# Norms of the heads' outputs: repeated over the channels by products, or as rows that a DMA repeats

## The chip, the cores and the metric

The kernel runs on one core of a Trainium2 chip. The metric is device time in microseconds of one execution. The engines that matter are TensorE (PE, with its weight loads as PEld), VectorE (DVE), ScalarE (ACT), GpSimd (POOL) and SyncE (SP), which here does nothing but issue DMAs, in the order of its queue.

## The reference, cut to what matters

A block with two layers over 768 tokens: 512 latent ones and 256 of a context, 1024 channels wide. Each layer projects a normed input into four groups of four heads each (windowed attention with a sink, "swa"; retention, "ret"; RWKV-7, "rwkv"; latent attention, "mla"), joins their outputs, projects them with `w_out`, and runs an MLP. The outputs of the retention and RWKV heads go through a norm over the 64 channels of each head, and this is what the change touches:

```python
def head_norm(o, gain, eps):
    mu = jnp.mean(o, axis=-1, keepdims=True)
    var = jnp.mean(jnp.square(o - mu), axis=-1, keepdims=True)
    y = (o - mu) * lax.rsqrt(var + eps)
    return y.reshape(o.shape[:-2] + (-1,)) * gain.astype(jnp.float32)
...
    def finish(o, gate):                                    # retention
        y = head_norm(o.transpose(0, 2, 1, 3), gn_g, RET_EPS)
        return (y * jax.nn.silu(gate.astype(jnp.float32))).astype(gate.dtype)
```

The kernel has the mean taken out of the weights beforehand, so only the factor rsqrt(mean of squares + eps), one number for each head and token, is left to be made and multiplied in.

## The kernel before

**Stages.** For each layer `l` the class Block runs `mixers` (projections and the RWKV recurrence), `attention` (L653), `out` (the product with `w_out`) and `mlp`. Data lies with channels on the partitions (two heads of 64 channels to a tile of 128 partitions) and tokens along the row. Layer 0 works on six tiles of 128 tokens, layer 1 on the four latent ones.

**What sets the order.** The program is recorded in the order in which it is written, and a scheduler then orders each engine's instructions, with the written order as priority. `merge` (L112) interleaves generators: it always advances the one whose yielded costs are the smallest share of the total that was given for it. In `attention` three streams run so: `mla` (total 58000), `swa` (54000), and `rest` (44000; all three times 0.84 in layer 1). `rest` is a chain: `finish` of RWKV (two pairs of heads, p = 0, 1), `ret` (two pairs, hp = 0, 1), and `w_out(l, 0)`, which loads the first half of the columns of `w_out` in eight pieces of 256 KB into the two buffers called wraw and splits each into a high and a low part, `wo` (an ACT cast at L209 and a subtraction by DVE or POOL at L212). `out` does the same for the second half. The yields of `rest` sum to 44200 in layer 0.

**PSUM.** In this stage there are two single banks (`pr`) and three pairs of banks (`ptok`); `done` gives one back. Three token tiles of the product with `w_out` are under way at a time, one in each pair.

**The norm.** `head_rstd` (L242) takes the squares `sq` of a pair of heads (`fsq` in `finish`, `rsq` in `ret`). `head_sums` sums them over each head by products with a 128x2 selector, scales on DVE (L237) and raises to the power -0.5 on POOL (L239): `hr`, tokens on the partitions, 2n columns for n token tiles. Then `on_channels` (L249) brings each column to 64 partitions by a product: a column of `hr`, broadcast to 64, as the stationary operand, and the identity as the moving one. That is 2n products into a pair of banks, for two `finish` and two `ret` pairs in each layer, 80 products in all (12 to each of four calls in layer 0, 8 to each in layer 1). DVE reads the result from PSUM right behind: at L1775 in `finish` and at L1032 in `ret`.

**Names.** `hrr` is a tile for transposed norms, `rstd` a DRAM row that `normalise` (L1438) already uses in the `mixers` stage: transpose, copy, DMA to DRAM, and DMAs that read each row back to 64 partitions. `prob` and `pt` are the probabilities of both attentions and their transposes, `y` the inputs of `w_out`. "D" is a pool of 17 tiles of 128x2x768, "B" one of 16 of 128x1024. `gate`, `gain` and `x` are rows that `out` needs behind its product. PE records each fp32 product as two.

## Time and profile before

| | us |
|---|---|
| median of 3 runs | 2207.34 (2202.97 to 2211.09) |
| the profiled execution: its own time | 2198.7 |
| the profiled execution: its span | 2196.9 |
| PE busy | 2057.8 (94%) |
| DVE busy | 1297.1 (59%) |
| ACT busy | 808.9 |
| POOL busy | 634.8 |
| mean granted clock of TensorE | 0.977 of full speed |

All stage times below are taken in the profiled execution, whose own time is 1.8 us over its span and 8.6 us under the median. Its first layer's `attention` streams run from 453 to 634.7 us and its product with `w_out` from there to 704 us; the second layer's run from 1630 to 1781.7 us and to 1824 us.

### The profile page before, as it was taken

Reading aid. Unit: us, or ns where it says so; the run is one execution under the profiler, and the core shown is the slowest. Engines: PE = TensorE matmul, PEld = TensorE weight load, DVE = VectorE, ACT = ScalarE, POOL = GpSimd, SP = SyncE. Lnnn points to the kernel's source line nnn. Section 1 sums busy time; section 2 is a strip of 40 time slices with the busy share of each in tenths; the row PEclk is TensorE's granted clock in tenths of the full one; section 3 lists DMA queues with packets and bytes.
Section 4 is the critical chain, followed back from the end, with each engine's and each line's share of the span. In section 5 each row is a group of like instructions: output and inputs, shape, how many; then the busy total and the mean of one; then the engine's idle time right before and its main releaser. Section 6 shows DMA issues by size and latency. Waiting matters only on the chain. (4 is left out here: it accounts for less than half of the span.)

```text
span 2196.9 us, 36212 instructions
## 1 busy us (share of the span) xinstructions
PE 2057.8 (94%) x14420; PEld 1616.1 (74%) x14420; DVE 1297.1 (59%) x2256; ACT 808.9 (37%) x1504; POOL 634.8 (29%) x679
## 2 busy tenths in 40 slices
PE   7988999988999999999999898999998899999997
PEld 4865766656768888888888677566666677888886
DVE  5478687677755756656555655666566645333334
ACT  3244444354444422222221333444454444322321
POOL 2542333331123311112211354333341123222321
PEclk9999999989899999999999999999998999999999
DMA  7233333522134444444443422111341133322332
GB/s 275 81 119 97 104 112 106 159 81 87 30 109 145 142 136 148 134 139 138 129 128 103 154 80 87 55 51 59 92 136 36 63 121 129 114 88 91 103 113 96
DMA packets 110885, 239.88 MB, mean 109 GB/s; under 512 B 22834, under 2 KB 49276, under 8 KB 110716
## 3 DMA queue, kind: packets, MB, share of 16 engines
q1 hardware_dynamic: 110716, 237.57, 33.5%
q8 instruction: 113, 1.85, 0.3%
q14 instruction: 56, 0.46, 0.1%
HBM read 206.93 MB, written 30.58 MB: 108 GB/s over the span
## 5 line engine op out<-in xcount | busy, mean ns | idle before, releaser
L150 PE MATMUL ps<-y,whi 128*128 128x512 f32 (+1 forms) x1664 | 420.9, 342 | 3.6 <-POOL y L493 2.3
L150 PE MATMUL ps<-whi,f 128*128 128x512 f32 x1280 | 399.5, 390 | 3.3 <-DVE f L1202 3.3
L209 ACT CAST whi<-wraw 128x1024 fp32r<-128x1024 f32 (+1 forms) x176 | 182.5, 1042 | 589.6 <-PE ps L150 364.6
L150 PE MATMUL ps<-hT,whi 128*128 128x512 f32 (+3 forms) x1360 | 381.4, 363 | 2.7 <-POOL hT L493 1.2
L150 PEld LDWEIGHTS ps<-y,whi 128*128 128x128 f32 x1664 | 289.0, 189 | 44.1 <-POOL y L493 4.1
L150 PE MATMUL ps<-y,wlo 128*128 128x512 f32 (+1 forms) x832 | 282.8, 341 | 0.6 <-POOL wlo L212 0.6
L150 PEld LDWEIGHTS ps<-whi,f 128*128 128x128 f32 x1280 | 240.2, 188 | 57.3 <-DVE f L1202 4.1
L150 PEld LDWEIGHTS ps<-hT,whi 128*128 128x128 f32 (+1 forms) x1360 | 234.8, 190 | 64.1 <-issue 24.3
L212 POOL TENSOR_TENSOR wlo<-wraw,whi 128x1024 fp32r<-128x1024 f32 x57 | 142.0, 2491 | 434.6 <-ACT whi L209 344.8
L150 PE MATMUL ps<-wlo,f 128*128 128x512 f32 x640 | 249.3, 390 | 0.0
L212 DVE TENSOR_TENSOR wlo<-wraw,whi 128x1024 fp32r<-128x1024 f32 x117 | 149.9, 1284 | 163.0 <-ACT whi L209 162.9
L150 PE MATMUL ps<-hT,wlo 128*128 128x512 f32 (+1 forms) x648 | 232.6, 359 | 0.0
L426 DVE SCALAR_TENSOR_TENSOR aacc<-aw,sil,aacc 128x768 f32<-128x768 f32 x140 | 159.8, 1188 | 30.1 <-ACT aacc L424 20.5
L150 PEld LDWEIGHTS ps<-y,wlo 128*128 128x128 f32 x832 | 157.3, 189 | 18.8 <-POOL wlo L212 0.8
L1201 POOL TENSOR_TENSOR fr<-fr 128x768 f32<-128x768 f32 (+1 forms) x64 | 91.3, 1427 | 271.3 <-ACT f L1200 263.1
L150 PEld LDWEIGHTS ps<-hT,wlo 128*128 128x128 f32 x648 | 124.8, 193 | 22.0 <-issue 7.2
L150 PEld LDWEIGHTS ps<-wlo,f 128*128 128x128 f32 x640 | 120.2, 188 | 24.4
L1202 DVE TENSOR_TENSOR f<-fr,f 128x768 fp32r<-128x768 f32 (+1 forms) x64 | 63.5, 992 | 121.4 <-POOL fr L1201 121.4
L1228 DVE TENSOR_TENSOR ya<-ya,ps 128x1024 f32<-128x1024 f32 x60 | 73.1, 1218 | 98.6 <-PE ps L150 98.6
L150 PE MATMUL ps<-wo,y 128*128 128x512 f32 x480 | 118.2, 398 | 2.9 <-POOL wo L212 2.7
L150 PEld LDWEIGHTS ps<-wo,y 128*128 128x128 f32 x480 | 87.7, 188 | 25.9 <-POOL wo L212 6.0
L1676 POOL TENSOR_SCALAR T<-rwvt 64x128 f32<-64x128 f32 x96 | 61.6, 643 | 74.1 <-PE ps L150 68.3
(306 smaller groups left out, 3231.2 us busy)
## 6 DMA issues: line engine op xcount, KB each, us to landing
wraw<-in_w_b_dram SPq DMA_DIRECT2D x64, 512.0 KB
wraw<-in_mlp_w_dram SPq DMA_DIRECT2D x64, 512.0 KB
aw<-in_ada_w_dram SPq DMA_DIRECT2D x80, 384.0 KB
wraw<-in_w_in_b_dram SPq DMA_DIRECT2D x46, 512.0 KB
ada<-in_ada_w_dram SPq DMA_DIRECT2D x64, 192.0 KB
adaw<-in_ada_s_dram SPq DMA_DIRECT2D x16, 512.0 KB
wraw<-in_w_out_k_dram SPq DMA_DIRECT2D x32, 256.0 KB
xs<-x SPq DMA_DIRECT2D x16, 512.0 KB
```

The costliest lines, as they stand in the source:

```text
L150: ins = self.nc.tensor.matmul(ps, lhsT, rhs, start=start, stop=stop, **kw).ins
L209: ins = self.nc.scalar.copy(hi, src)
L212: (lo_eng or self.nc.vector).tensor_tensor(lo, src, hi.bitcast(F32), ALU.subtract)
L426: nc.vector.scalar_tensor_tensor(a, w, sil, a, ALU.mult, ALU.add)
L1201: nc.gpsimd.tensor_tensor(fr, fr, fr, ALU.mult)
L1202: nc.vector.tensor_tensor(fl, fr, fh.bitcast(F32), ALU.subtract)
L1228: nc.vector.tensor_tensor(ya[t], ya[t], ps, ALU.add)
L1676: nc.gpsimd.tensor_scalar(T3[r, par, dr], self.vt[r, gc[dr]], 1.0, None, ALU.mult)
```

## The change

`head_rstd` no longer calls `on_channels`. It transposes `hr` by one product into a single bank, copies that to `hrr` on ACT, writes it to a DRAM row, and reads the row back twice, each time repeated over 64 partitions, into the tile that held the squares. The users of the norm become functions `last`, put on a list `ends`, and are emitted later: by `end()` in `finish` behind the squares of the next pair, in `ret` behind the token-major copy of v of the next pair, and for the last pair by `at_end()`, which comes behind `w_out(l, 0)`. The yields change (1500 more in each `head_rstd`, less elsewhere), so `rest` sums to 48200, with its total left at 44000.

```diff
@@ -239,12 +239,23 @@
         nc.gpsimd.tensor_tensor(r, r, self.mhalf[:, 0:1].broadcast_to([128, 2 * nt * nb]), ALU.pow)
         return r
 
-    def head_rstd(self, sq, tiles, mul, add, add_op):
-
-        n = len(tiles)
+    def head_rstd(self, sq, tiles, mul, add, add_op, name):
+
+
+        n, t0 = len(tiles), 128 * tiles[0]
         r = self.head_sums([sq], tiles, mul, add, add_op)
         yield 400.0 * n
-        return self.on_channels(lambda j, t: r[:, n * j + t - tiles[0]:n * j + t - tiles[0] + 1], 2, tiles)
+        pt = self.pr(128)
+        self.tp(pt[0:2 * n], r, self.cc("ident"))
+        rr = self.mp.tile([24, 128], F32, tag="hrr", name="hrr", bufs=1)
+        self.nc.scalar.copy(rr[0:2 * n], pt[0:2 * n])
+        self.done(pt)
+        dd = self.dr.tile([2, 128 * n], F32, name=name)
+        self.nc.sync.dma_start(dd.rearrange("r (t x) -> (r t) x", x=128), rr[0:2 * n])
+        for j in range(2):
+            self.nc.sync.dma_start(sq[64 * j:64 * j + 64, t0:t0 + 128 * n], dd[j].partition_broadcast(64))
+        yield 1500.0
+        return sq[:, 0:T]
 
     def on_channels(self, col, n, tiles):
 
@@ -653,9 +664,19 @@
     def attention(self, l, emit):
         merge((self.rw.tail(), 16.0), (self.mla_prep(l, emit), 14e3), (self.swa_prep(l, emit), 4e3))
         self.rebank(2, (2, 4, 6))
-        rest = chain(self.rw.finish(), self.ret(l, emit), self.w_out(l, 0))
+        self.ends = []
+        rest = chain(self.rw.finish(), self.ret(l, emit), self.w_out(l, 0), self.at_end())
         streams = [(self.mla(l, emit), 58000.0 * (1.0 if emit else 0.84)), (self.swa(l, emit), 54000.0 * (1.0 if emit else 0.84)), (rest, 44000.0 * (1.0 if emit else 0.84))]
         merge(*streams)
+
+    def end(self):
+
+        while self.ends:
+            self.ends.pop(0)()
+
+    def at_end(self):
+        self.end()
+        yield 1
 
     def ypair(self, key):
         self.y[key] = self.D("y", F32R)
@@ -952,6 +973,11 @@
         ch = lambda x: x.rearrange("p (c i) -> p c i", i=128)
         rep = lambda x: x.unsqueeze(1).broadcast_to([128, nch, 128])
         cjx = lambda x: x.rearrange("p (c j x) -> p c j x", j=2, x=64)
+
+        def last(hp, o, rs):
+            nc.vector.tensor_tensor(o, o, rs, ALU.mult)
+            self.put_y(*self.ypair(("ret", hp)), tq0, T - tq0, o)
+
         for hp in range(2):
             qk, qd, gv = [self.D("ret") for _ in range(3)]
             q, k, g = qk[:, 0], qk[:, 1], gv[:, 0]
@@ -966,6 +992,7 @@
             nc.sync.dma_start(g[:, tq0:], s["ret"][4 + hp][:, tq0:])
             v = self.token_major(gv[:, 1], gv[:, 1], "cent")
             yield 1300
+            self.end()
             ps = self.ptok()
             for t in range(6):
                 self.tp(ps[:, 128 * t:128 * t + 128], k[:, 128 * t:128 * t + 128], self.cc("ident"))
@@ -1026,12 +1053,8 @@
             o = self.B("ro")[:, 0:T]
             nc.vector.scalar_tensor_tensor(o[:, tq0:], po[:, tq0:], d["ret_gn_g"][:, hp:hp + 1], gate, ALU.mult, ALU.mult)
             self.done(po)
-            rs = yield from self.head_rstd(sq, list(range(c0, 6)), 1.0 / 64, 1e-5, ALU.add)
-            yield 200.0
-            yh, yl = self.ypair(("ret", hp))
-            nc.vector.tensor_tensor(o[:, tq0:], o[:, tq0:], rs[:, tq0:], ALU.mult)
-            self.done(rs)
-            self.put_y(yh, yl, tq0, T - tq0, o[:, tq0:])
+            rs = yield from self.head_rstd(sq, list(range(c0, 6)), 1.0 / 64, 1e-5, ALU.add, f"retn{l}{hp}")
+            self.ends.append(lambda hp=hp, o=o[:, tq0:], rs=rs[:, tq0:]: last(hp, o, rs))
 
 
     def gate_row(self, l, s, off, gname):
@@ -1758,6 +1781,19 @@
         sg, gup = sx[:, 0], sx[:, 1, 0:256]
         nc.sync.dma_start(sg[:, tq0:], self.dsg[:, tq0:])
         nc.sync.dma_start(gup, K.I["rwkv_g_up"][self.l])
+
+        def last(p, of, bo, rs):
+            y = of[:, tq0:]
+            nc.vector.scalar_tensor_tensor(y, y, d["rwkv_gn_g"][:, p:p + 1], rs[:, tq0:], ALU.mult, ALU.mult)
+            nc.vector.tensor_tensor(y, y, bo[:, tq0:], ALU.add)
+            yh, yl = K.ypair(("rwkv", p))
+            for t0, n in segs:
+                ps = K.pr(n)
+                K.mm(ps, gup[:, 128 * p:128 * p + 128], sg[:, t0:t0 + n], True, True)
+                nc.vector.tensor_tensor(of[:, t0:t0 + n], of[:, t0:t0 + n], ps, ALU.mult)
+                K.done(ps)
+                K.put_y(yh, yl, t0, n, of[:, t0:t0 + n])
+
         for p in range(2):
             (of, ob), (bo, bs) = ([x[:, 0], x[:, 1]] for x in [K.D("fin") for _ in range(2)])
             nc.sync.dma_start(of[:, tq0:], self.do[0][:, p, tq0:])
@@ -1769,20 +1805,10 @@
             sq = K.B("fsq")
             nc.scalar.activation(sq[:, tq0:T], of[:, tq0:], AF.Square)
             yield 500
-            rs = yield from K.head_rstd(sq, list(range(tq0 // 128, 6)), 1.0 / 64, 64e-5, ALU.add)
-            yield 200.0
-            y = of[:, tq0:]
-            nc.vector.scalar_tensor_tensor(y, y, d["rwkv_gn_g"][:, p:p + 1], rs[:, tq0:], ALU.mult, ALU.mult)
-            K.done(rs)
-            nc.vector.tensor_tensor(y, y, bo[:, tq0:], ALU.add)
-            yh, yl = K.ypair(("rwkv", p))
-            for t0, n in segs:
-                ps = K.pr(n)
-                K.mm(ps, gup[:, 128 * p:128 * p + 128], sg[:, t0:t0 + n], True, True)
-                nc.vector.tensor_tensor(of[:, t0:t0 + n], of[:, t0:t0 + n], ps, ALU.mult)
-                K.done(ps)
-                K.put_y(yh, yl, t0, n, of[:, t0:t0 + n])
-            yield 1300
+            K.end()
+            rs = yield from K.head_rstd(sq, list(range(tq0 // 128, 6)), 1.0 / 64, 64e-5, ALU.add, f"rwkn{self.l}{p}")
+            K.ends.append(lambda p=p, of=of, bo=bo, rs=rs: last(p, of, bo, rs))
+            yield 700
 
 
 _INS = ["x", "c", "ctx", "c_ctx", "ada_w", "ada_b", "post_mix_g", "post_mlp_g", "swa_sink", "rwkv_w0", "rwkv_w_up",
```

PE, where the first norm of layer 0 is made: the piece of the difference with the first products of `hr` (`cst,hr`), among those of `swa` and `mla` (`skh,sq`, `mqk`, and the transposes `cst,prob`).

```order
 L150 MATMUL ps<-cst,fsq 128x2 x6
 L150 MATMUL ps<-cst,prob 128x128 x2
-L150 MATMUL ps<-cst,hr 64x128 x3
 L150 MATMUL ps<-skh,sq 128x256
 L150 MATMUL ps<-skl,sq 128x256
-L150 MATMUL ps<-cst,hr 64x128
 L150 MATMUL ps<-mqk 128x256
-L150 MATMUL ps<-cst,hr 64x128
 L150 MATMUL ps<-cst,prob 128x128 x2
-L150 MATMUL ps<-cst,hr 64x128 x3
 L150 MATMUL ps<-skh,sq 128x256
+L150 MATMUL ps<-cst,prob 128x128 x2
```

Eight of the twelve products are gone in this piece, the other four a little later; what stands in their place, one transposition `ps<-cst,hr 12x128`, comes 13 rows behind it.

ACT, at the end of layer 0's `attention`, before (L674 and L696 are softmax and transposed probabilities, L713 the outputs `y`):

```order
L674 ACTIVATE prob,nm<-ps,nm,rq 128x768
L713 CAST y<-ps 128x128
L209 CAST wo<-wraw 128x512
L696 COPY pt<-ps 128x384 x2
L209 CAST wo<-wraw 128x512 x2
L713 CAST y<-ps 128x128
L209 CAST wo<-wraw 128x512 x10
```

The same place now, with line numbers of the changed kernel:

```order
L251 COPY hrr<-ps 12x128
L717 COPY pt<-ps 128x384
L695 ACTIVATE prob,nm<-ps,nm,rq 128x768
L209 CAST wo<-wraw 128x512
L734 CAST y<-ps 128x128
L717 COPY pt<-ps 128x384 x2
L209 CAST wo<-wraw 128x512
L734 CAST y<-ps 128x128
L209 CAST wo<-wraw 128x512
L734 CAST y<-ro 128x768
L209 CAST wo<-wraw 128x512 x13
```

Six of the sixteen `wo` casts stood ahead of the last `y` of `attention`, and now two do; the cast of the last retention pair (`y<-ro`) moved behind that `y`. In layer 1 it is six before and four now. On PE, 16 products with `wo` stood ahead of the end of this stage in layer 0 and 17 in layer 1, and now 8 and 9 do.

SP, the DMA issues at the same place, before:

```order
L1111 DMA wraw<-in_w_out_k_dram 128x512
L1041 DMA gate<-mod_88 128x1024
L1042 DMA gain<-in_post_mix_g_dram 128x1024
L1041 DMA gate<-mod_88 128x1024
L1042 DMA gain<-in_post_mix_g_dram 128x1024
L1086 DMA x<-in_x_dram 128x1024
L1111 DMA wraw<-in_w_out_k_dram 128x512 x14
```

And now:

```order
L254 DMA retn_5876<-hrr 12x128
L256 DMA rsq<-retn_5876 64x768 x2
L1134 DMA wraw<-in_w_out_k_dram 128x512 x2
L1064 DMA gate<-mod_88 128x1024
L1134 DMA wraw<-in_w_out_k_dram 128x512
L1065 DMA gain<-in_post_mix_g_dram 128x1024
L1134 DMA wraw<-in_w_out_k_dram 128x512
L1064 DMA gate<-mod_88 128x1024
L1134 DMA wraw<-in_w_out_k_dram 128x512
L1065 DMA gain<-in_post_mix_g_dram 128x1024
L1134 DMA wraw<-in_w_out_k_dram 128x512
L1109 DMA x<-in_x_dram 128x1024
```

The loads of `gate`, `gain` and `x` stood ahead of fourteen of the loads of `w_out`, and now stand among them, behind the DMAs of the last norm.

## Rows read from the trace of the kernel before

**Rows 1.** The page: PE's busy time, and the chain that ended last, by line

```profile
PE 2057.8 (94%) x14420; PEld 1616.1 (74%) x14420; DVE 1297.1 (59%) x2256; ACT 808.9 (37%) x1504; POOL 634.8 (29%) x679
...
PE ps L150 14%; DVE sq L1057 0%; DVE x L1060 0%; DVE ya L1088 0%; ACT sq L1090 0%; DVE f L1202 0%; POOL wlo L212 0%; POOL fr L1201 0%; POOL rs L224 0%; POOL rs L223 0%; ACT f L1200 0%; ACT fr L1198 0%; POOLq L1831 0%; ACTq L1831 0%; POOLq L1043 0%
```

**Rows 2.** Windows: length, busy PE, PEld, DVE, ACT, POOL, clock, DMA, GB/s; the stages

```profile
453.00:634.70 181.70, 163.88 (x1249) 121.48 (x1247) 132.70 (x350) 86.92 (x227) 34.50 (x21) 0.92 0.23 71
634.70:704.00 69.30, 68.38 (x312) 54.35 (x311) 31.28 (x45) 26.68 (x48) 19.12 (x29) 1.00 0.44 152
1630.00:1781.70 151.70, 133.52 (x1019) 99.25 (x1017) 104.23 (x265) 68.65 (x163) 25.80 (x18) 0.92 0.20 64
1781.70:1824.00 42.30, 41.46 (x178) 32.44 (x178) 16.53 (x21) 14.86 (x25) 11.98 (x14) 1.00 0.48 162
```

**Rows 3.** PE's waits (us, times, longest), layer 0's stage, then one of layer 1

```profile
PE ps L150 <- ACT prob L674: 5.8, 6, 2.2
PE ps L150 <- POOL hr L239: 4.5, 3, 1.9
...
PE ps L150 <- POOL hr L239: 3.2, 4, 1.3
```

**Rows 4.** The tile hr (ns min/median/max, start): products in layer 0, layer 1, POOL

```profile
L150 PE MATMUL ps<-cst,hr x96: 272/283/477, 473.6 to 610.8; 128*64 128x128 f32 x96
...
L239 POOL TENSOR_TENSOR hr<-hr,mhalf x4: 2264/2264/2289, 471.2 to 606.4; 128x12 f32<-128x12 f32 x4
...
L150 PE MATMUL ps<-cst,hr x64: 272/370/477, 1654.2 to 1758.8; 128*64 128x128 f32 x64
```

**Rows 5.** Timeline of PE (start, us, records): the first call's products

```profile
473.56 0.65 PE L150 MATMUL ps<-cst,hr 128*64 128x128 f32 x6 [1.93 <-POOL hr L239]
474.14 0.55 PE L150 MATMUL ps<-skh,sq 128*128 128x256 f32 x1
...
484.38 0.67 PE L150 MATMUL ps<-cst,hr 128*64 128x128 f32 x8
484.98 1.56 PE L150 MATMUL ps<-fin 128*128 128x512 f32 x4
```

**Rows 6.** Windows, columns as in 2, where the clock fell

```profile
472.00:488.00 16.00, 14.44 (x73) 9.73 (x73) 8.59 (x32) 6.75 (x24) 1.50 (x1) 0.68 0.00 1
...
500.00:508.00 8.00, 7.66 (x72) 5.80 (x73) 3.00 (x8) 1.79 (x5) 0.49 (x2) 0.79 0.01 2
...
1672.00:1680.00 8.00, 6.99 (x29) 4.53 (x30) 3.23 (x9) 2.92 (x8) 0.95 (x1) 0.57 0.24 74
```

**Rows 7.** Timelines of DVE and SP: normalise()'s way, layer 1

```profile
1309.21 0.27 DVE L1449 COPY hrr<-ps 24x128 f32<-24x128 f32 x1
...
1318.59 0.96 DVE L1457 TENSOR_TENSOR rwkh<-rwkh,ksq 128x768 f32<-128x768 f32 x1 [2.86 <-DMA ksq<-rstd]
...
1309.51 0.32 SPq L1452 DMA_DIRECT2D rstd<-hrr  x1
...
1313.15 2.39 SPq L1455 DMA_DIRECT2D ksq<-rstd  x4
```

**Rows 8.** Timeline of ACT: last y, last wo cast, both layers

```profile
634.73 0.26 ACT L713 CAST y<-ps 128x128 fp32r<-128x128 f32 x1
...
655.29 0.62 ACT L209 CAST wo<-wraw 128x512 fp32r<-128x512 f32 x1 [0.82 <-DMA wraw<-in_w_out_k_dram]
...
1781.61 0.27 ACT L713 CAST y<-ps 128x128 fp32r<-128x128 f32 x1 [0.87 <-PE ps L150]
...
1801.64 0.62 ACT L209 CAST wo<-wraw 128x512 fp32r<-128x512 f32 x1 [1.26 <-DMA wraw<-in_w_out_k_dram]
```

**Rows 9.** Timeline of PE: the products with wo, layer 0

```profile
634.72 8.05 PE L150 MATMUL ps<-wo,y 128*128 128x512 f32 x33
642.96 12.30 PE L150 MATMUL ps<-wo,y 128*128 128x512 f32 x50 [0.19 <-POOL wo L212]
```

**Rows 10.** Window, columns as in 2: gate, gain and x loads in layer 0

```profile
608.00:616.00 8.00, 6.75 (x67) 4.76 (x68) 7.39 (x15) 4.59 (x12) 3.52 (x3) 1.00 0.63 199
```

## The prediction

> **What bounds the kernel now.** I read the page first: TensorE is busy 94% of the span and the chain that ended last lies almost wholly on it [rows 1], so only what shortens PE's stream counts. Then the windows by stage [rows 2]. The change touches the two `attention` stages, 181.70 and 151.70 us long. PE is busy 90% and 88% there, DVE 73% and 69%, and the clock is 0.92. PE is thus the bound, but with gaps, and the next row view, PE's waits [rows 3], says who makes them: in layer 0 the softmax's `prob` (5.8 us) and POOL's `hr` (4.5 us), in layer 1 `hr` 3.2 us. Behind each of these stages comes the product with `w_out`, where PE is busy 98.7% and 98.0% [rows 2]: what is pushed over the end of `attention` costs its full length.
>
> **The change part by part.**
>
> *Products taken away.* 48 products in layer 0 and 32 in layer 1, 96 and 64 records [rows 4]. Their durations overlap, so I take the distance from the start of a group to the start of the next instruction. In the first call [rows 5] six records take 474.14 - 473.56 = 0.58 us at a low clock and eight take 484.98 - 484.38 = 0.60 at full clock; with its three groups between, the call comes to 3.45 us. Read in the same way the other three calls of layer 0 give 2.09, 3.22 and 1.86, those of layer 1 1.91, 1.90, 1.38 and 1.02: 16.8 us in all. As a lower bound, 160 records at 0.60/8 = 0.075 us are 12.0. PE is busy nine tenths of the stage, so I count nine tenths of 16.8: **-15.1** (bounds -12.0 and -16.8).
>
> *PE's wait for POOL.* The power on POOL takes 2.26 us in layer 0 [rows 4], and PE stood for it 4.5 + 3.2 = 7.7 us [rows 3]. Now only one transposition waits for it, and the order puts it 13 rows further back. The next to come late is `prob`, which is the largest wait already; I let it take a fifth back: **-6.2** (bounds 0, if `prob` sets the pace anyway, and -7.7).
>
> *Transpositions.* Eight, each one product of `hr`. The removed ones cost 16.8/80 = 0.21 us each on average, 0.15 to 0.29 between the groups at full clock and the first call's mean: 8 x 0.21 = **+1.7** (1.2 to 2.3).
>
> *The single bank.* The transposition holds one of two single banks until ACT has copied it. ACT is busy 48% of the stage [rows 2], so the copy may stand behind one exponential of about 1 us, and the transposes of `pt` use the same two banks. No row shows this; bounds are 0 and 8 x 1.0 = 8, and against it a pair of banks, held until DVE had read it, comes free. Since the other bank stays, I take **+1.0**.
>
> *The way through DRAM.* A copy, a write, two reads for each call, 24 DMAs on SP. The nearest rows are `normalise`'s [rows 7]: the copy starts at 1309.21, the write is issued at 1309.51, the reads at 1313.15, and DVE's use starts at 1318.59 after a wait of 2.86 us for it: 9.4 us, with four reads and a weight load in between; with two reads I put 6.5 to 9.4. The users are emitted one step of `rest` later. For the first pair of `finish` they stand, in the order and by the times of before, some 20 us behind the copy, so this costs nothing there. What covers it is the next pair's work; without cover it would cost DVE, and everything queued behind that multiply there (the maxima and sums of both softmaxes), up to 9.4 us for each of eight calls. The last retention pair has only what is left of `w_out`'s splits: by the order its copy would fall near 625.6 and its rows land near 635, at the end of the stage, where the cast `y<-ro` is queued on ACT ahead of thirteen `wo` casts. In layer 1 its multiply stands ahead of the last two copies of `pt` on DVE, 0 to 3 us early. I take 0 here; the bound is +3.
>
> [...]
>
> *What the later end of `rest` moves.* `rest` now yields 48200 against a total of 44000, so five of the splits are left when `mla` has ended, instead of two. In layer 0, two of sixteen `wo` casts stand ahead of the last `y` instead of six, in layer 1 four instead of six; and PE has 8 products with `wo` fewer to fill its gaps with in each layer. One costs 12.30/50 = 0.246 us [rows 9], so 2 x 8 x 0.246 = **+4.0** of work moves into stages that are full of PE (bounds 0 and 4.0). The splits themselves are late. Ten casts took 655.29 - 634.73 = 20.6 us in layer 0 and 1801.64 - 1781.61 = 20.0 in layer 1, paced by DMA [rows 8]: 2.06 and 2.0 each, so four and two late ones are 4 x 2.06 + 2 x 2.0 = 12.2 us. Against that, three token tiles interleave: PE first needs the last split at the 130th product in layer 0, 32 us after its start at 0.246 each, and 14 casts at 2.06 are done after 29. It just holds. And `gate`, `gain` and `x` load among these splits now: three loads of 512 KB moved in 608 to 616 us at 199 GB/s and a DMA share of 0.63 [rows 10], so at a full share one takes 524288 B / 316 GB/s = 1.7 us; five in layer 0 and three in layer 1 are 13.3 us of DMA. The stage had a DMA share of 0.44 [rows 2], so most of it finds room. For late splits and loads together I take **+2.0** (bounds 0 and 12.2 + 13.3 = 25.5).
>
> Sum: -15.1 - 6.2 + 1.7 + 1.0 + 4.0 + 2.0 = **-12.6** against the profiled execution's 2198.7, so 2186.1. The median of before is 2207.34/2198.7 = 1.0039 of that execution; in its terms the forecast is 2194.7.
>
> **The rivals.**
>
> *The clock.* In layer 0, the two falls at 472 to 488 (0.68) and 500 to 508 (0.79) begin right behind waits for `hr` of 1.9 and 1.8 us, and in layer 1 that at 1672 to 1680 (0.57) follows another [rows 6]. What was lost in them is 16 x 0.32 + 8 x 0.21 + 8 x 0.43 = 10.2 us. If these falls go with the waits, the change is -22.8, which is 2184; with no cost at the tail -28.8, 2178. Against it: other falls follow waits for `prob`, and a stream with fewer products may only fall elsewhere. [...]
>
> *The gain is absorbed.* PE is 10% idle in these stages, and the round trip from scores through DVE and ACT back to PE sets their pace at places [rows 3]. If it does so throughout, products that are gone only turn into longer waits for `prob`: I leave a third of the -21.3, -7.1, and with +5 of costs it is -2 to -7: 2200 to 2205.
>
> *The tail, slower than before.* If PE runs out of splits behind the end of `attention`, the late casts (12.2) and the loads among them (13.3) show in full: -21.3 + 2.7 + 4.0 + 25.5 = +10.9, which is 2218. It decides at the pace of the splits: at over 2.4 us for each instead of 2.06, 14 casts take longer than the 32 us that three interleaved tiles last. For it: DMA already ended most of the casts' idle times [rows 8]. Against it: PE did not wait for more than 0.19 us for a `wo` in the rows of before, with the same tiles interleaved [rows 9].
>
> *DVE waits for rows.* If a multiply comes to the head of DVE's queue before its row has landed, at the last pair of each layer or where the streams run faster than the scheduler thought, two to four calls at about 3 us give back 6 to 12: -6.6 to -0.6, 2200 to 2207.
>
> **How the numbers follow.** About 0.5% (11 us) is what a measurement of this kernel can tell from no change. Chances: my forecast (-5 to -20) 0.50, of which 0.33 lie beyond -11; the clock 0.14; absorbed 0.18; the tail 0.11, nearly all of it between 0 and +11; DVE's wait 0.07. Faster by over 0.5%: 0.33 + 0.14 = 0.47. Slower by over 0.5%, the upper end of the tail: 0.06. The rest is 0.47 within; since unnamed costs go that way, I move 0.05 of it to slower. The range leaves out the far half of the clock's case and the last of the tail's: 2178 to 2214.
>
> **What would show it.** In the trace after: no records of 64 columns from `hr`, and eight transpositions; no wait of PE for `hr` over 0.5 us; PE's busy time in the two `attention` stages down by 12 to 17 us and the stages shorter by nearly that. Copy to use of the rows by DVE 6.5 us or more, with no wait for them on DVE but at the last pair. In the `w_out` stages, waits of PE for `wo` under 2 us. I am wrong if PE's waits for `prob` grow by what the products save, if the granted clock of the stages leaves 0.92, or if PE waits for `wo` by 5 us or more behind `attention`.

## The result: slower by 0.56%

The changed kernel takes 2216.89 us in the median (2213.82 to 2219.91, 6 runs) against 2206.53 of the kernel before beside it: a ratio of 1.0056, 95% interval 1.0040 to 1.0073. Forecast was 2194.7, range 2178 to 2214. The profiled execution has a span of 2215.6 us, 18.7 more than the one of before, which was a run below that kernel's median. Four executions of the kernels in the experiments, two of no_rows and one each of pow_halves and rows_unread, took 2323 to 6732 us and are in none of the figures.

TensorE's busy time, from the page:

```profile
PE 2062.0 (93%) x14268; PEld 1614.2 (73%) x14268; DVE 1304.0 (59%) x2256; ACT 810.3 (37%) x1512; POOL 635.8 (29%) x679
```

PE's busy time is 4.2 us higher [rows 1], though 80 products are gone. The stages say how that can be (columns as in rows 2; I let each window begin at the same instruction as there: `attention` of layer 0, the stage of `w_out`, then the same for layer 1):

```profile
456.20:635.40 179.20, 157.93 (x1149) 116.52 (x1147) 129.95 (x347) 85.25 (x226) 28.75 (x18) 0.90 0.21 63
635.40:715.00 79.60, 72.97 (x320) 57.01 (x321) 33.48 (x48) 29.74 (x52) 25.35 (x32) 0.98 0.51 173
1643.00:1791.30 148.30, 131.73 (x950) 97.19 (x948) 105.74 (x264) 68.07 (x165) 22.09 (x16) 0.91 0.20 62
1791.30:1835.60 44.30, 43.28 (x185) 33.82 (x184) 15.90 (x18) 15.03 (x26) 13.96 (x14) 1.00 0.56 186
```

Against [rows 2], `attention` is 2.5 us shorter in layer 0 (179.20 for 181.70) and 3.4 in layer 1. PE's busy time there fell by 6.0 and 1.8 us only, and the clock from 0.92 to 0.90 and 0.91. A product at the low level is busy for longer: in the changed kernel twelve sums of `fsq` take 1.40 us at 472.75, where the clock is 1.00, and 2.72 at 498.36, where it is 0.50. Idle time of PE went from 17.8 to 21.3 us in layer 0. Who makes it (PE's waits, layer 0, then layer 1):

```profile
PE ps L150 <- DVE pt L715: 3.6, 2, 3.2
PE ps L150 <- DVE fin L1793: 2.6, 1, 2.6
PE ps L150 <- DVE mqk L838: 2.6, 2, 2.1
PE ps L150 <- DVE rS L1024: 2.6, 1, 2.6
PE ps L150 <- ACT kt L1004: 2.0, 2, 1.4
PE ps L150 <- ACT prob L695: 2.0, 6, 0.7
...
PE ps L150 <- ACT prob L695: 4.4, 3, 2.4
PE ps L150 <- DVE fin L1793: 2.4, 2, 2.2
PE ps L150 <- ACT fsq L1806: 2.3, 1, 2.3
```

The 7.7 us of waits for POOL's `hr` [rows 3] are gone, as forecast, and the waits for `prob` even shrank in layer 0. In their place stand `fin`, `pt`, `kt`, `rS` and, in layer 1, `fsq`. That the edit does what it says (the tile hr in layer 0, and the copy to hrr):

```profile
L239 POOL TENSOR_TENSOR hr<-hr,mhalf x4: 2267/2278/2307, 474.4 to 621.0; 128x12 f32<-128x12 f32 x4
...
L150 PE MATMUL ps<-cst,hr x4: 269/272/275, 482.4 to 626.6; 128*12 128x128 f32 x4
...
L251 ACT COPY hrr<-ps x8: 238/255/256, 484.3 to 1780.7; 12x128 f32<-12x128 f32 x4, 8x128 f32<-8x128 f32 x4
```

Four transpositions where there were 96 records of products [rows 4], and eight copies.

Behind `attention` the gain is lost. PE's waits in layer 0's stage of `w_out`, then its first and last group of products there, and a wait of layer 1 behind its own stage:

```profile
PE ps L150 <- ACT v L500: 2.8, 1, 2.8
PE ps L150 <- DVE sq L1080: 1.2, 1, 1.2
PE ps L150 <- ACT wo L209: 1.0, 1, 1.0
PE ps L150 <- POOL wo L212: 1.0, 3, 0.4
...
635.50 1.88 PE L150 MATMUL ps<-wo,y 128*128 128x512 f32 x7
...
693.95 18.44 PE L150 MATMUL ps<-wo,y 128*128 128x512 f32 x80
...
1842.36 1.15 PE L150 MATMUL ps<-cst,sq 128*128 128x128 f32 x4 [5.40 <-ACT v L500]
```

The answering rows of before, the end of the same products and the same place in layer 1:

```profile
682.11 19.32 PE L150 MATMUL ps<-wo,y 128*128 128x512 f32 x84
...
1825.53 0.44 PE L150 MATMUL ps<-cst,sq 128*128 128x128 f32 x2 [1.10 <-ACT v L489]
```

From the end of `attention` to the last product with `wo` it was 701.4 - 634.7 = 66.7 us and is 712.4 - 635.4 = 77.0, so +10.3. In layer 1 the stage is 2.0 longer by the windows, and behind it PE waits 5.4 us for the normed rows (`v`) where it waited 1.1; counted from the end of that stage, the first product of its MLP comes 5.2 us later than before and its later ones 6.6. The sum over the two profiles: -2.5 - 3.4 + 10.3 + 2.0 + 6.6 = +13.0; 3.2 us lie ahead of the change, in code that is the same, and the rest is spread.

### The profile page after: what moved, and what is told of

It is laid out like the page before. It is cut to its first block, busy times and chain, and to the rows that moved or that the text cites. A ratio compares the mean times of both kernels' runs of the same rounds, so it can differ in the third digit from the quotient of the medians.

```text
span 2215.6 us, 35951 instructions
## 1 busy us (share of the span) xinstructions
PE 2062.0 (93%) x14268; PEld 1614.2 (73%) x14268; DVE 1304.0 (59%) x2256; ACT 810.3 (37%) x1512; POOL 635.8 (29%) x679
## 5 line engine op out<-in xcount | busy, mean ns | idle before, releaser
L1645 ACT COPY Xp<-Yt 32x256 f32<-32x256 f32 x192 | 77.4, 403 | 12.7 <-DVE Yt L1643 6.5
```

Of the source, the lines that this page charges most:

```text
L1645: nc.scalar.copy(Xp[r, :, b], Yt[r])
```

## Two parts of the time

Every run lists its span and its mean granted clock, and the profile of the changed kernel shows the clock at two levels, full and half: in windows of 1 us around one of its falls (495 to 509 us) it is 1.00 or 0.50, but for the two in which it changes (0.85 and 0.74), and over the whole span it is 1.00 in 2057 windows, 0.50 in 108 and between them in 50 (before: 2079, 82 and 35). So a span splits into low time, 2 x (1 - clock) x span, half of which is lost where work takes twice as long, as those twelve sums nearly do, and a rest, span - low/2, that would then be left at full clock; that all of the low time goes at half pace is an estimate. Before, for instance: 2 x 0.0236 x 2201 = 104 us low, and a rest of 2149.7. Means over the runs that the comparisons use, ratios with their 95% interval, each against the runs of before that were taken beside the kernel:

| kernel | runs | median | ratio to before | low, us | rest, us |
|---|---|---|---|---|---|
| before | 121 | 2203.2 | | 104 | 2149.7 |
| after | 6 | 2216.9 | 1.0056 (1.0040 to 1.0073) | 134 | 2148.0 |
| no_products | 12 | 2204.7 | 0.9986 (0.9964 to 1.0007) | 124 | 2138.2 |
| products_twice | 7 | 2218.9 | 1.0060 (1.0037 to 1.0082) | 111 | 2159.4 |
| const_products | 9 | 2188.2 | 0.9937 (0.9914 to 0.9960) | 87 | 2144.9 |
| products_later | 9 | 2207.1 | 1.0032 (1.0014 to 1.0051) | 121 | 2147.3 |
| defer_products | 12 | 2209.2 | 1.0024 (1.0013 to 1.0035) | 112 | 2150.8 |
| pow_halves | 11 | 2199.6 | 0.9993 (0.9979 to 1.0007) | 96 | 2150.9 |
| pow_quarters | 12 | 2201.2 | 0.9985 (0.9973 to 0.9998) | 91 | 2153.6 |
| order_only | 12 | 2208.4 | 1.0026 (1.0008 to 1.0043) | 117 | 2148.3 |
| late_only | 6 | 2232.0 | 1.0116 (1.0096 to 1.0136) | 140 | 2160.4 |
| after_pace | 6 | 2222.8 | 1.0069 (1.0047 to 1.0091) | 145 | 2147.4 |
| after_fill | 6 | 2219.4 | 1.0088 (1.0065 to 1.0110) | 128 | 2155.3 |
| after_pace_fill | 6 | 2218.5 | 1.0076 (1.0053 to 1.0099) | 133 | 2150.5 |
| after_act_queue | 12 | 2217.5 | 1.0050 (1.0030 to 1.0069) | 133 | 2147.8 |
| rows_at_once | 4 | 2247.2 | 1.0203 (1.0187 to 1.0220) | 177 | 2156.3 |
| finish_rows | 6 | 2216.2 | 1.0067 (1.0049 to 1.0086) | 142 | 2144.1 |
| ret_rows | 6 | 2214.6 | 1.0060 (1.0043 to 1.0078) | 117 | 2154.8 |
| no_rows | 10 | 2192.7 | 0.9955 (0.9940 to 0.9970) | 102 | 2140.3 |
| rows_unread | 11 | 2201.8 | 0.9987 (0.9971 to 1.0003) | 111 | 2143.6 |

The changed kernel's rest is 1.7 us better than before; its low time is 30 us longer, which costs 15. That split is arithmetic, not yet a cause. Within the kernel before the low time scatters by about 9 us from run to run (one standard deviation), so a mean of six runs is good to some 4 us; in no_products and const_products it scatters by 18, so their means of 12 and 9 runs are good to 5 and 6. The stage figures above come from one profile of each kernel, so they are one sample.

## Experiments: what the products are worth

The theories that the expectations name: A, the loss lies in the late end of `rest`; B, in the rows' way through SP and DRAM; C, the gain is absorbed by other waits; D, it is given back by the clock, if that falls when PE has less to do or waits more; E, PE has slack and another round trip sets the pace; F, any change of the order moves the time.

**no_products** leaves the products out, and with them the norm's factor; so do const_products, no_rows and rows_unread below. These four price parts of the work and compute another result.

```diff
-        return self.on_channels(lambda j, t: r[:, ...], 2, tiles)
+        return sq[:, 0:T]
-            self.done(rs)        # in ret, and K.done(rs) in finish
```

> The kernel before without the 80 products that spread hr over the channels: their users read the squares in SBUF instead, so the norm's factor is left out of the result and nothing waits for POOL's hr. What all of it is worth, at no cost in its place. If PE bounds the stage as my sum had it, -15.1 - 6.2 = -21 us: 2184 to 2188. If other waits take the place of what is removed (theory C), -5 to -10: 2196 to 2201.

Measured 2204.66, ratio 0.9986: no gain, which neither forecast had. The rest fell by 11.5 us, for the products and PE's waits for POOL together; the low time rose by 20 us, which gives 10 of them back. Its profile has the clock at 0.86 in layer 0's `attention` (windows of the two `attention` stages):

```profile
454.50:642.80 188.30, 167.96 (x1151) 123.56 (x1147) 134.96 (x350) 86.68 (x227) 35.54 (x21) 0.86 0.21 69
1639.20:1784.30 145.10, 128.90 (x953) 95.45 (x952) 105.00 (x265) 67.81 (x163) 25.87 (x18) 0.92 0.21 67
```

**products_twice** makes each product twice.

```diff
+                for _ in range(n):
-                self.mm(ps[m * j:m * j + m, ...], col(j, t)..., True, True)
+                    self.mm(ps[m * j:m * j + m, ...], col(j, t)..., True, True)
```

> The kernel before with each of the 80 products made twice into the same place, 16.8 us more of PE work by the trace. If PE is the bound as in my sum, +15 us: 2219. Theory D (clock): the added work stands behind the same waits and keeps the clock up, so at most half of it shows, +2 to +8: 2206 to 2212. Theory E (slack): within 4 us of before.

Measured 2218.93, +16 us in the median; rest +9.7, low +7. So the price of the products at full clock is about 10 us when they are added, and at most 11.5 when they are taken out. Theory D's reading that added work would half pay for itself does not hold here.

**const_products** keeps them but lets them depend on nothing.

```diff
-        return self.on_channels(lambda j, t: r[:, ...], 2, tiles)
+        return self.on_channels(lambda j, t: self.mhalf[:, 0:1], 2, tiles)
```

> The kernel before with its 80 products kept in their places, but their stationary operand is a constant column instead of a column of hr, so PE waits for no POOL (the norm's factor is left out of the result). Without the products there was no gain at all, and the granted clock of the profiled attention of layer 0 was low for 51 us instead of 27. Theory D, the clock: PE's own work keeps its clock up, so with the work kept and the waits gone the low stretches shrink, and this is 5 to 15 us faster than before, 2189 to 2199, faster than with the products left out. Theory E, other engines' round trip is what paces the stage and PE's work has slack in it: same as before and as without products, 2200 to 2208. If PE is the bound as in my sum, -6: about 2198.

Measured 2188.17, ratio 0.9937. The same `attention` windows:

```profile
451.30:630.70 179.40, 168.30 (x1248) 124.53 (x1246) 132.68 (x350) 86.08 (x226) 34.56 (x21) 0.90 0.23 72
1629.40:1773.10 143.70, 128.59 (x1017) 95.97 (x1015) 104.19 (x265) 68.41 (x162) 26.04 (x18) 0.96 0.21 67
```

Against no_products this kernel has the 80 products more, and is 16 us faster: its rest is 6.7 us longer and its low time 37 us shorter. In layer 0 PE is idle 11.1 us here and 20.3 there, where it waits longer for `pt`, `kt` and `mqk`. Less work, longer waits and another order go together in this pair, and it doesn't show which of them lowers the clock. That the work alone doesn't decide it is seen below: in the order of the change, the kernel without products has the shorter low time (no_rows, 102 us, against defer_products, 112).

## Experiments: the wait for POOL by itself

Four kernels keep the computation whole and only keep PE from waiting for the power.

**products_later**, the products a longer step behind the sums:

```diff
-        yield 400.0 * n
+        yield 1000.0 * n      # and the total of rest 58400 for 44000
```

> The kernel before with products and use in their order, but the yield between the sums and the products 2.5 times as long (1000 n for 400 n) and the total of rest raised with it to 58400, so that PE does other work while POOL makes hr. By the order, 10 to 25 rows of other products now stand between. Theory D: PE's 7.7 us of waits for hr go, the low time shrinks as with products of a constant: 5 to 12 us faster than before, 2191 to 2198. If the wait only moves to the softmax, 2199 to 2208.

**defer_products**, products and use behind the next pair's first steps, as in the change but without rows (shown against the kernel before, cut):

```diff
-        return self.on_channels(lambda j, t: r[:, ...], 2, tiles)
+        return lambda: self.on_channels(lambda j, t: r[:, ...], 2, tiles)
# called in last(), which end() runs as in the change; at_end() ahead of w_out
```

> The other half of the change alone: the norms are still spread by products of hr, but products and users are emitted behind the next pair's first steps (the last pair's ahead of the splits of w_out), so PE finds hr long done and waits for no POOL. No row goes through DRAM; the yields sum to 43400 against the total of 44000, so rest isn't late. Theory D (clock): like the products of a constant, 5 to 15 us faster than before: 2189 to 2199. Theory E: 2200 to 2208. If holding the D tiles longer delays the loads of ret on SP (theory B), slower than before by 4 or more.

**pow_halves** and **pow_quarters**, the power in two or four parts, each with its tile (hrp), the code cut:

```diff
-        nc.gpsimd.tensor_tensor(r, r, mhalf..., ALU.pow)
+        for j in range(2):        # 4 in pow_quarters
+            nc.gpsimd.tensor_tensor(h[j], r[:, nt * j:nt * j + nt], mhalf..., ALU.pow)
```

> The kernel before with POOL's power of each norm made in two halves into two small tiles, the products of the first head of the pair ahead of those of the second, so that PE can start when half of the power is done (1.1 instead of 2.3 us in layer 0). Nothing else is changed. By the kernel with products of a constant (no wait: -14 us), theory D says that shorter waits also shrink the low time: 4 to 10 us faster than before, 2193 to 2199. If the gain of that kernel came from something else than the wait: 2200 to 2207.

> The kernel before with POOL's power of each norm in four parts (three columns each in layer 0, two in layer 1) into four small tiles, the products in the order in which the parts are made: PE can start after about 0.7 us instead of 2.3. If the wait for POOL is what the products of a constant saved (theory D), PE's waits for the power fall under 1.5 us and the time by 6 to 12: 2191 to 2197. If that kernel's gain came with its order, as others moved by 5 us with theirs: 2198 to 2204.

The first two came out slower, 2207.1 and 2209.2. The parted powers gave 2199.6 and 2201.2, a gain of 1.5 and 3.3 us by the ratios, less than the 5 us that an exchange of neighbours moves (order_only, below). PE's waits did fall as meant (pow_halves, layer 0 and layer 1; then pow_quarters, layer 0):

```profile
PE ps L150 <- POOL hrp L242: 1.9, 3, 1.0
...
PE ps L150 <- POOL hrp L242: 1.2, 2, 0.6
```

```profile
PE ps L150 <- ACT prob L685: 7.2, 6, 2.2
...
PE ps L150 <- POOL hrp L243: 0.9, 2, 0.7
```

From 7.7 us to 3.1 and, with 0.7 in layer 1, to 1.6, and the low time from 104 to 96 and 91. But `prob` took 7.2 for 5.8 [rows 3], and the rest grew by 1 and 4 us. So in none of these four orders did cutting the wait for POOL give more than about 3 us, and of the 15 us of const_products most has another source, which I can't name: in that kernel PE waits for nothing in the norm but 0.3 us for the scaled sums in layer 0.

## Experiments: the late end of rest

**late_only** makes `rest` late in the kernel before; **after_pace** makes it early in the changed one; **order_only** shifts the same number by 1%.

```diff
-        streams = [..., (rest, 44000.0 * ...)]
+        streams = [..., (rest, 39000.0 * ...)]   # late_only, on before
+        streams = [..., (rest, 48000.0 * ...)]   # after_pace, on after
+        streams = [..., (rest, 44400.0 * ...)]   # order_only, on before
```

> The kernel before with one number changed: the total given for the stream rest is 39000 instead of 44000, so its end, the splits of w_out, comes late as in the changed kernel (2 instead of 6 wo casts ahead of the last y of layer 0, 7 instead of 16 products with wo ahead of the end of the stage). The products of hr and their use stay. Theory A, the loss lies in the late end of rest: 10.3 + 0.6 us in layer 0 and 1.9 + 6.7 in layer 1 behind attention, 19.5 in the profiles, so this is slower than before by 10 to 20 us, 2217 to 2227. Theory B, the loss comes from the rows' way through SP and DRAM: within 4 us of before. Theory C, the gain is only absorbed and the tail costs the 6 us of my sum: 2210 to 2214.

> The changed kernel with one number changed: the total given for rest is 48000 instead of 44000, as its yields have grown from 44200 to 48200. By the order, 5 instead of 2 wo casts then stand ahead of the last y of layer 0, and 16 instead of 8 products with wo ahead of the end of the stage, as in the kernel before. Theory A (late end of rest): most of the 19.5 us behind attention comes back, 10 to 18 us faster than the changed kernel: 2199 to 2207. Theory B (rows' way): at most 4 us faster, 2213 to 2217. Theory C (absorbed, tail 6 us): 2208 to 2213.

> The kernel before with the total given for rest 44400 instead of 44000, under 1% more. No instruction is added or removed and the tail stays (five instead of six wo casts ahead of the last y in layer 0, 17 products with wo ahead of the end instead of 16); only neighbours change places here and there. It tells how far any reordering moves the time: Theory F, the order itself is worth as much as what the change gained or lost: 5 us or more from before, either way. Theories A, D, E: within 4 us of before, 2200 to 2208.

late_only lost 28 us, more than theory A said. after_pace should then have won and did not: 2222.79. Its windows (layer 0, the stage of `w_out` up to the last product with `wo`, layer 1):

```profile
451.80:636.70 184.90, 161.34 (x1155) 120.11 (x1151) 131.11 (x349) 87.93 (x230) 32.47 (x20) 0.89 0.23 72
636.70:706.20 69.50, 65.55 (x291) 52.04 (x292) 29.96 (x42) 24.88 (x43) 21.46 (x30) 1.00 0.48 168
1636.60:1792.00 155.40, 138.61 (x959) 99.68 (x957) 102.86 (x264) 68.02 (x166) 23.26 (x17) 0.88 0.22 68
```

The tail of layer 0 did come back, 69.5 us for 77.0, and `attention` took it: 184.9 and 155.4 us for 179.2 and 148.3, at a clock of 0.89 and 0.88. Theory A doesn't hold for the changed kernel: there the early end only moves time from one stage to another. order_only shows the ground on which all of this stands: exchanging neighbours, with nothing added, moved the time by 5 us, nearly all of it low time (117 for 104).

**after_fill** and **after_pace_fill** put 80 products of a constant back on PE, read by nobody:

```diff
         yield 400.0 * n
+        self.done(self.on_channels(lambda j, t: self.mhalf[:, 0:1], 2, tiles))
         pt = self.pr(128)
```

> The changed kernel with 80 products of a constant column put back on PE where the products of hr stood; nothing reads them. Over all executions so far, time splits into a part at full clock and half of the time at the low level: before 2149.5 us and 105 us low, the changed kernel 2148.0 and 134, the kernel before without its products 2138.2 and 124, with products of a constant 2144.9 and 87. Theory D (clock): the added 12 us of work at full clock bring 15 to 30 us of low time back to full, so this is no slower than the changed kernel: 2206 to 2219. If PE's work has no hand in its clock, 12 us are added: 2226 to 2231.

> As the last, and with the total of rest at 48000, so that the splits of w_out come as early as before. Theory D: the low time of the changed kernel at that pace was 145 us, the highest of all; with the products of a constant put back it falls to 100 to 120, and with the tail as before the time is 2203 to 2213. If the clock is not a matter of PE's work: 2222.8 + 12, about 2233.

2219.4 and 2218.5. The fill cost 7 us of rest in the first and 3 in the second, and gave back 6 and 12 us of low time. So 80 products on PE are nearly free there, but they don't bring the clock of before back: in the changed kernel, missing work is not what makes most of the low time.

## Experiments: the rows' way

**after_act_queue** moves the DMAs of the rows from SP to ACT:

```diff
-        self.nc.sync.dma_start(dd..., rr[0:2 * n])
+        self.nc.scalar.dma_start(dd..., rr[0:2 * n])     # the two reads likewise
```

> The changed kernel with the 24 DMAs of the rows issued from ACT's queue instead of SP's, so that the loads of finish and ret on SP stand behind none that waits for hrr. In the profile of the changed kernel PE waits 2.6 + 2.4 us for the sum fin and 2.3 for its square, which it did not before. Theory B (queue of SP): 5 to 10 us faster than the changed kernel, 2207 to 2212. Theories A and C: within 4 us of it, 2213 to 2221, ACT's own queue being held up by the issues at most.

2217.45, as the changed kernel. The queue of SP is not the cause. One wait of this kernel bears on what follows, PE's for DVE's multiply by the gate, in layer 0:

```profile
PE ps L150 <- DVE fin L1793: 0.4, 1, 0.4
```

**rows_at_once** uses the rows without deferral, with the yields of before:

```diff
-        return self.on_channels(lambda j, t: r[:, ...], 2, tiles)
+        ...            # transposition, copy, write, two reads, as in the change
+        return sq[:, 0:T]
```

> One half of the change alone: rows through DRAM instead of products, but the use emitted at once and the yields and totals of before. DVE's multiply then waits for its row, 6.5 to 9 us after the copy, with whatever the scheduler queued behind it. If those waits hold DVE up (my fourth rival), slower than the changed kernel, 2220 to 2235, most of it as waits of DVE for the rows. If the scheduler has put enough ahead of them, the deferral is not what matters, and the time lies with the changed kernel and the one without products: 2203 to 2218, with a low time of 115 to 135 us by theory D.

2247.21, the slowest of all. DVE's wait for the rows in layer 0, PE's largest wait there, then the first trip: the copy, the use by DVE, and the piece of PE's wait that answers it:

```profile
DVE fin L1784 <- DMA fsq<-rwkn: 7.1, 2, 4.3
...
PE ps L150 <- DVE fin L1790: 13.4, 2, 6.7
...
482.24 0.24 ACT L251 COPY hrr<-ps 12x128 f32<-12x128 f32 x1
...
488.11 1.02 DVE L1784 SCALAR_TENSOR_TENSOR fin<-fin,prm,fsq 128x768 f32<-128x768 f32 x1 [2.79 <-DMA fsq<-rwkn]
...
490.97 1.11 PE L150 MATMUL ps<-cst,prob 128*128 128x128 f32 x4 [6.70 <-DVE fin L1790]
```

DVE waits 7.1 us, but PE 13.4. The reason is in PE's rows: `last` multiplies the result by a gate, whose products (`ps<-fin`) need no row. They run early, at 480.58 and 482.96, and take both single banks; DVE frees these only when the row has come and the multiplies ahead are done, by its multiplies at 490.22. Until then PE has no bank for a transpose, and its next product starts at 490.97. From the copy to a use that waited for its row it is 488.11 - 482.24 = 5.9 us here. In the changed kernel it is 576.10 - 568.57 = 7.5 us at the one use that waited.

In the changed kernel the gate's products hold the banks too, but not because a row is missing. Its first trip (copy on ACT, write and reads on SP, the use on DVE, and DVE's multiply that frees the banks):

```profile
484.27 0.24 ACT L251 COPY hrr<-ps 12x128 f32<-12x128 f32 x1
...
484.54 0.31 SPq L254 DMA_DIRECT2D rwkn<-hrr  x1
485.88 1.61 SPq L256 DMA_DIRECT2D fsq<-rwkn  x2
...
493.57 1.01 DVE L1787 SCALAR_TENSOR_TENSOR fin<-fin,prm,fsq 128x768 f32<-128x768 f32 x1
...
497.63 1.01 DVE L1793 TENSOR_TENSOR fin<-fin,ps 128x512 f32<-128x512 f32 x2
```

and PE at that place, with the clock around it:

```profile
491.51 1.02 PE L150 MATMUL ps<-fin 128*128 128x512 f32 x2
...
492.96 0.60 PE L150 MATMUL ps<-fin 128*128 128x256 f32 x2
...
498.36 2.72 PE L150 MATMUL ps<-cst,fsq 128*128 128x2 f32 x12 [2.63 <-DVE fin L1793]
...
488.00:496.00 8.00, 7.74 (x46) 5.24 (x42) 7.55 (x21) 5.37 (x14) 0.00 (x0) 1.00 0.10 26
498.00:506.00 8.00, 7.38 (x42) 5.93 (x43) 2.97 (x10) 2.88 (x7) 2.27 (x1) 0.59 0.23 74
```

The gate's products run at 491.51 and 492.96, the banks come free behind 497.63, and PE waits 2.63 us. DVE did not wait for the row: its use at 493.57 has no idle time ahead of it, so the 9.3 us from the copy are the place of the use in DVE's order and not the length of the trip. Right behind PE's wait the clock is at 0.59, from 1.00 ahead of it, and the twelve sums take 2.72 us: with this wait went some 8 x 0.41 = 3.3 us more. But waits for this multiply come to 2.6 + 2.4 us only in the changed kernel's two layers, and after_act_queue, with 0.4 in layer 0 and none in layer 1, takes as long. The held banks explain rows_at_once; they are not what makes the changed kernel's loss.

**no_rows** takes the way out of the changed kernel and keeps deferral, yields and totals; **rows_unread** keeps the way and takes the dependence out; its reads bring 256 columns, where those of the change bring 768 in layer 0 and 512 in layer 1.

```diff
-        pt = self.pr(128)
-        ...                       # no_rows: transposition, copy and DMAs gone
-            self.nc.sync.dma_start(sq[64 * j:64 * j + 64, t0:t0 + 128 * n], dd[j]...)
+            self.nc.sync.dma_start(sq[64 * j:64 * j + 64, T:1024], dd[j][0:256]...)  # rows_unread
```

> The changed kernel without transposition, copy and the three DMAs of each norm: the users read the squares themselves (the norm's factor is left out of the result); deferral, yields and totals are those of the changed kernel. If the rows' way (queues, waits for rows) makes the loss: 8 to 15 us faster than the changed kernel, at the 2204.7 of the kernel before without its products, 2202 to 2209. If the deferral and the late end of rest make it: within 5 us of the changed kernel, 2212 to 2222.

> The changed kernel with its whole way through DRAM (transposition, copy, write, two reads repeated over 64 partitions), but the reads put 256 of the columns into the unused end of the squares' tile, and the users read the squares (the norm's factor is left out of the result). So all instructions and DMAs are there, 24 on SP as in the changed kernel, and only the users' dependence on the rows is gone. If that dependence makes the loss (users and with them y, gate and gain later): near no_rows, 2193 to 2201. If the way itself makes it (the transposition on PE, the copy on ACT, the single bank, the queue of SP): near the changed kernel, 2211 to 2220.

no_rows: 2192.7, 24 us faster than the changed kernel and 10 faster than before (ratio 0.9955). rows_unread: 2201.8, in the middle. Windows of no_rows (layer 0, its stage of `w_out`, layer 1), and of rows_unread (the two `attention` stages):

```profile
459.10:624.40 165.30, 146.41 (x1142) 108.92 (x1140) 131.21 (x348) 85.62 (x224) 34.14 (x21) 0.95 0.22 73
624.40:699.70 75.30, 69.97 (x302) 54.92 (x303) 30.44 (x43) 26.12 (x45) 19.76 (x29) 0.98 0.43 151
1629.40:1767.90 138.50, 123.58 (x943) 90.74 (x942) 103.76 (x264) 66.54 (x160) 24.55 (x17) 0.95 0.20 65
```

```profile
454.00:632.40 178.40, 159.49 (x1147) 119.19 (x1144) 131.88 (x348) 86.44 (x229) 35.32 (x22) 0.89 0.22 72
1639.40:1777.10 137.70, 121.96 (x946) 90.14 (x944) 100.73 (x262) 66.13 (x162) 24.49 (x16) 0.96 0.21 70
```

The way's instructions thus cost 9 us (rest +3, low +10), and the users' dependence on the rows another 15 (rest +4, low +23), as far as two other orders can tell it. The dependence also moves the users: 664 instructions of DVE stand ahead of the first multiply of `finish` in rows_unread and no_rows, 723 in the changed kernel; ahead of the first of `ret` it is 854 and 887. And no_rows has the late tail too, 75.3 us for 66.7 before, yet it is the second fastest kernel. The late end of `rest` moves time between stages; it doesn't decide the sum.

The windows of no_rows and of the changed kernel also say what kind of time the 24 us are. The two `attention` stages are 179.20 - 165.30 = 13.9 and 148.30 - 138.50 = 9.8 us longer with the rows, which is all of the difference of the two profiles (22.4 us). PE's idle time there grew by 2.4 and 1.7 us only, while the clock fell from 0.95 to 0.90 and 0.91: by length times (1 - clock), this costs 17.9 - 8.3 and 13.3 - 6.9, together 16 us. So most of the loss is PE's own work at the low level, and not waiting. Which waits or gaps let the clock fall is not shown.

**finish_rows** and **ret_rows** make one half of the change each:

```diff
-            rs = yield from K.head_rstd(...)          # ret_rows: finish as before,
+            rs = yield from K.head_rstd_old(...)      # total 46600; finish_rows: ret as before, 45400
```

> Half of the change: rows through DRAM and deferred use in finish, products as before in ret; the total of rest is raised with its yields (45400). The tail of the stage is as before by the order (five wo casts ahead of the last y in layer 0, 18 products with wo). If the loss of the changed kernel lies at the end of rest, this half is free of it and lies with the kernel before, -4 to +4: 2199 to 2207. If holding the tiles of finish longer and the later loads on SP make the loss: +6 to +13, 2209 to 2216.

> The other half: products as before in finish, rows and deferred use in ret, the last pair's behind w_out's splits; the total of rest raised with its yields (46600). If the loss lies with the last pair of ret at the end of rest: most of it stays, +8 to +15, 2211 to 2218. If it lies in finish: -4 to +4, 2199 to 2207.

2216.2 and 2214.6: each half alone loses what the whole does (ratios 1.0067 and 1.0060, the whole 1.0056). finish_rows loses in low time (142 for 104, the rest 5.6 better), ret_rows about as much in the rest (+5.1) as in low time (+13, which costs 6.5). So the loss is no sum of costs per norm; why two halves together lose no more than one stays open.

## Why the prediction was wrong, point by point

- *The way through DRAM, with the transpositions and the single bank: 0 + 1.7 + 1.0.* This is the step that failed. The sum put the way at 0 because the next pair's work would cover the trip, and the trip is covered: DVE waits for a row once, 2.1 us. Yet no_rows against the changed kernel has +24 us for the way and the dependence, where the sum had +2.7; rows_unread parts it into 9 for the instructions and 15 for the dependence. I looked for waits, and there are few: PE's idle time in the two stages is 4.0 us above that of no_rows, and the clock, 0.90 and 0.91 for 0.95, makes some 16 us. No term of the sum stood for that. The bound of 8 for the bank was looked for at the transposition; where a bank does hold PE up, it is held for the user (rows_at_once, 13.4 us in layer 0). The length of the trip was put at 6.5 to 9.4 us and is 5.9 (rows_at_once) and 7.5 (the changed kernel) where a use waits for its row.
- *Products, -15.1.* They are worth 6.7 us at full clock (const_products against no_products) to 9.7 (products_twice), and at most 11.5 with the waits for POOL (no_products). The distances that I summed contain stretches of low clock; the bound of 12.0 was the better figure.
- *That this gain shows in the time.* In the order of before it does not: no_products has 20 us more low time and no gain. I took the stage's clock of 0.92 as given in the sum and gave the clock a rival of its own with a gain only. In the order of the change it does show: no_rows, with neither products nor rows, is 10 us faster than before, where the sum without the rows' terms had -15.1 - 6.2 + 4.0 + 2.0 = -15.3, and it is 16 us faster than defer_products, which defers in the same way and keeps the products.
- *The wait for POOL, -6.2.* The waits went; what cutting them gave was at most 3 us (pow_halves, pow_quarters), nearer the bound of 0.
- *Late splits, +6.0.* Behind `attention` the profile has +10.3, +2.0 and +6.6. PE's waits for `wo` were 2.0 us in layer 0, as I had them. The rest goes at least in part to the tiles' norms, which follow one another behind the last split (waits for `v` and `sq` of 2.8, 1.2 and 5.4 us), a chain that I had not costed. It is not what decides, by after_pace and no_rows.
- *The rivals.* The tail's 2218 is near the measured time by luck: its mechanism, PE out of splits with the loads in full, is not what happened. The gain absorbed by `prob` is not seen either. DVE's wait for rows came once, 2.1 us; it is what rows_at_once shows (2247), where the use is not deferred. The clock came with the other sign, and of the prediction's signs of being wrong it is the one that came: 0.90 and 0.91 for 0.92. The runs show no single rule for it: without the products the low time is longer in no_products against const_products, 124 us against 87, and shorter in no_rows against defer_products, 102 against 112.

What stays open: why the low time of the changed kernel is 30 us longer than before. It is located in the rows' way by no_rows and in the two `attention` stages by the windows; the fall behind one wait is shown, and the rest is not added up. Of the kernels that compute the whole result, pow_quarters alone lies below before by its interval (0.9985, 0.9973 to 0.9998), by less than an exchange of neighbours moves.

## What to carry to other kernels

On a TensorE that is 90% busy with a wavering clock, what small products are worth depends on the order around them: taking the same 80 out gave nothing in one order and 16 us in another. So price each half of an edit by itself, by leaving it out: one kernel without the rows' way told that the loss lay there, where the list of waits did not. When a value goes through DRAM, ask not only how long the trip is, but where its user moves in its engine's order and what it holds until then (here PSUM banks). And exchange a few neighbours for nothing first: here that alone moves the time by 5 us, so a gain of that size needs more than one order to be believed.

## What the runs showed of the hardware

The low time of TensorE's clock differs between runs of the same kernel by about 9 us (one standard deviation, 121 runs of before, 2194 to 2214 us). Half of that, 4.5 us, is no less than the scatter of the time itself, 3.8 us, so much of the scatter of this kernel's time is its clock. 80 more products went with a faster kernel: 2188.2 with them, on a constant (const_products), and 2204.7 without (no_products). And a trip of 12 rows to DRAM and back, repeated over 64 partitions, took 5.9 us (rows_at_once) and 7.5 us (the changed kernel) from the copy ahead of it to a use that waited for it.
